# One order of the products for all wide weight chunks of a two-layer hybrid encoder trunk

## The chip, the cores and the metric

The kernel runs on one core of a Trainium2 chip. The metric is the device time of one execution in microseconds (us), taken as the median over several runs. The engines are TensorE (PE, with its weight loads PEld), VectorE (DVE), ScalarE (ACT), GpSimd (POOL) and SyncE (SP, which issues most DMAs).

## What is computed

The reference is a trunk of two layers over 256 frames of width 2048, in float32:

```
for layer in range(2):
    h = rms_norm(x, norm_mix_w[layer]) * (1 + sc1) + sh1        # scale, shift, gate from mod_w[layer] and c
    if layer == 0:
        mix = gdn_attn_mixer(h, ...)     # gated DeltaNet heads and chunked band attention, one output product
    else:
        mix = mamba2_ssd(h, ...)         # projections, convolution, SSD scan over chunks, gate, output product
    x = x + g1 * mix
    h = rms_norm(x, norm_mlp_w[layer]) * (1 + sc2) + sh2
    a = relu(h @ mlp_w1[layer])          # 2048 -> 8192
    x = x + g2 * ((a * a) @ mlp_w2[layer])   # 8192 -> 2048
```

Every large product is a stream of float32 weights against the 256 frames.

## The kernel before

All activations stay on the chip; weights come from HBM in chunks of 128 x 2048 numbers (1 MB), one DMA each. A chunk and the activations are each split in two float32r parts, a high one (the rounded value) and a low one (the rest), and three partial products are summed: high x high, high x low and low x high. For a chunk, `loader` (L467) issues the DMA on SP, ACT casts each half of the chunk to its high part `wh`, and DVE subtracts to get the low part `wl` (`split`, L317). There are four buffers of `wh` and four of `wl`, which is two chunks.

There are three kinds of items. `b_item` and `a_item` serve projections of 512 columns of weights; in `a_item` the weights are the moving operand and all its products are 512 columns wide. `c_item` (L559) serves a *wide chunk*: 256 columns of weights by 8 K tiles of 128. In it the weights are stationary. The moving operand is the activations: high and low part side by side, 512 columns, for `wh` (the function `both`), and the high part alone, 256 columns, for `wl` (the function `low`). So a wide chunk is 2 column tiles x 8 K tiles = 16 products of 512 columns and 16 of 256. The two column tiles `ct` add up in two different PSUM banks of one tile `pw`; the eight K tiles come in two halves `hf` of four, and each half has its own `wh` and `wl`.

Wide chunks in order of time: 16 of the output product of layer 0, 128 of its MLP, 24 of the SSD mixer's projections, 16 of its output product, again 24 and 16, and 128 of the MLP of layer 1; 352 in all. Between the two groups of projections and the output products stand the gate blocks of the SSD mixer (`a_item`).

What sets the order of the work is the program's own text and then a scheduler. The text runs one item after the other; `emit` (L242) loads the next item's weights and then runs the pending item, whose `run` yields every eight products. At each yield, `tick` (L227) lets background tasks step (evictions, convolutions, the SSD scan) and issues a share of the modulation weights' work (`mod_job`, L419: a DMA and a DVE step of 2.3 us). A scheduler then moves instructions within each engine's stream by its own estimates; so another order on PE can also change the order on DVE and ACT.

Which order the 32 products of a wide chunk take is `self.order`. It is "tile" outside the MLPs; inside them `mlp` (L1344) sets it anew for each of the eight half stages of each layer from a table (L1349). With W for a product of 512 columns and L for one of 256:

```
tile        W L W L ... within one half and one column tile
tile pairs  W W L L ... within one half and one column tile
row         W W L L ... column tiles in turn
crossed     W and L of both column tiles mixed
half        8 W, 8 L, 8 W, 8 L; four K tiles of one column tile, then of the other
half rows   8 W, 8 L, 8 W, 8 L; column tiles in turn
chunk rows  16 W, 16 L; column tiles in turn
```

In the gate blocks of the SSD mixer, two groups of each four set `self.flip` (L1579), which takes the two frame halves, and so the two PSUM banks, in turn.

Of the kernel before, what the change touches and what calls it, by code (L numbers as in the profile page):

```python
# [18 lines left out]
P = 128  # L19
# [93 lines left out]
class Trunk:  # L113
# [8 lines left out]
    def __init__(self, tc, ctx, ins, out):  # L122
        self.tc, self.nc = tc, tc.nc
        self.i, self.out = ins, out
        self.n = 0
        pool = lambda name, bufs, **k: ctx.enter_context(tc.tile_pool(name=name, bufs=bufs, **k))
        self.cp = pool("cp", 1)
        self.raw_p = pool("rawp", 4)
        self.w_p = pool("wp", 4)
        self.u_p = pool("up", 18)  # L130
        self.s_p = pool("sp", 2)
        self.dram_p = pool("drp", 1, space=bass.MemoryType.DRAM)
        self.ps_g = pool("psg", 2, space=PSUM)
        self.ps_m = pool("psm", 4, space=PSUM)
        self.fast, self.bg, self.open = [], [], []
        self.fast_n, self.bg_n = 0.5, 0.5
        self.credit = self.fcredit = 0.0
        self.pending = None
        self.order, self.flip = "tile", False
        self.pin = self.still = 0  # L140
        self.ahead = None
        self.pin_mod = 0
        self.debt = self.rate = 0.0
        self.modgen = iter(())
# [377 lines left out]
    def a_item(self, ps, src, act, first, last, after=None, whole=False):  # L522

        load, ws = self.loader(src, whole)
        flip = self.flip and not whole

        def run():
            o_, (u, x) = ps(), act()
            for hf, (wh, wl) in enumerate(self.tiles(ws, 512)):
                if flip:  # L530
                    for k in range(2):
                        ka = hf * 2 + k
                        st, sp = first and ka == 0, last and ka == 3
                        T = [slice(t * P, t * P + P) for t in range(2)]
                        for n in range(3):
                            for t in range(2):
                                self.mmx(o_[t], u[hf][:, k, n // 2, T[t]], (wh, wl, wh)[n][:, k], st and n == 0, sp and n == 2)
                        yield
                    continue
# [19 lines left out]
    def c_item(self, ps, src, act, first, last, after=None):  # L559

        load, ws = self.loader(src)

        order = self.order

        def run():
            o_ = ps()
            halves = self.tiles(ws, 256)

            def both(ct, hf, k):
                u = act(2 * hf + k // 2)[:, k % 2]  # L570
                self.mmx(o_[:, ct].rearrange("p a t -> p (a t)"), halves[hf][0][:, k, ct * P : ct * P + P], u.rearrange("p a t -> p (a t)"),
                         first and hf == k == 0, last and hf == 1 and k == 3)

            def low(ct, hf, k):
                self.mmx(o_[:, ct, 1], halves[hf][1][:, k, ct * P : ct * P + P], act(2 * hf + k // 2)[:, k % 2, 0], False, last and hf == 1 and k == 3)

            def steps(order):

                if order == "tile":
                    return [[f(ct, hf, k) for k in range(4) for f in (W, L)] for hf in range(2) for ct in range(2)]  # L580
                if order == "tile pairs":
                    return [[f(ct, hf, k + n) for k in (0, 2) for f in (W, L) for n in range(2)] for hf in range(2) for ct in range(2)]
                if order == "row":
                    return [[f(ct, hf, k + n) for n in range(2) for f in (W, L) for ct in range(2)] for hf in range(2) for k in (0, 2)]
                if order == "half":
                    return [[f(ct, hf, k) for ct in range(2) for k in range(4)] for hf in range(2) for f in (W, L)]
                if order == "half rows":
                    return [[f(ct, hf, k) for k in range(4) for ct in range(2)] for hf in range(2) for f in (W, L)]
                if order == "chunk rows":
                    return [[f(ct, hf, k) for k in range(4) for ct in range(2)] for f in (W, L) for hf in range(2)]  # L590
                if order == "crossed":
                    res = []
                    for hf in range(2):
                        a = [f for k in range(4) for f in ([W(0, hf, k)] + ([L(1, hf, k - 1)] if k else []) + [W(1, hf, k), L(0, hf, k)])] + [L(1, hf, 3)]
                        res += [a[:8], a[8:]]
                    return res

            W = lambda *a: (both, a)
            L = lambda *a: (low, a)
            for step in steps(order):  # L600
                for f, a in step:
                    f(*a)
                yield
# [740 lines left out]
    def mlp(self, layer, acts, after=None):  # L1344
# [4 lines left out]
        orders = ((("row", "tile pairs"), ("half", "half rows"), ("chunk rows", "crossed"), ("tile", "row")),  # L1349
                  (("tile pairs", "half"), ("half rows", "chunk rows"), ("crossed", "row"), ("half rows", "tile pairs")))  # L1350
# [14 lines left out]
        for f in range(NF):  # L1365
            a = []
            self.order = orders[layer][f][0]
# [5 lines left out]
            self.order = orders[layer][f][1]  # L1373
# [5 lines left out]
        self.order = "tile"  # L1379
# [6 lines left out]
    def run(self):  # L1386
# [176 lines left out]
        for half in range(2):  # L1563
# [14 lines left out]
            for g in G:  # L1578
                self.flip = g % 4 > 1  # L1579
                self.a_block(i["w_sz"], SZ + g, acts, lambda ps, g=g: os_.__setitem__(g % 4, self.evac(self.ssd_gate(g, ps, ys[g]), 1)))  # L1580
            self.flip = False
# [75 lines left out]
```

## Time and profile before

| | |
|---|---|
| median of 3 runs | 2752.32 us (2750.8 to 2754.2) |
| the profiled execution | 2751.96 us |
| its span, first to last instruction | 2750.2 us |
| PE busy | 2678.6 us |
| DVE busy | 2154.5 us |
| ACT busy | 1323.7 us |
| HBM read | 675.33 MB |

The rows further down name an instruction by line, engine, operation and tiles, out<-in. `pw` is the PSUM tile of a wide chunk; `pg` that of the other items; `pm` holds small products. `u` are activations, `wh` and `wl` the two parts of weights, `mraw` modulation weights, `sE`, `scb`, `sxw` tiles of the SSD scan. Matmuls are pipelined: the duration of one is longer than the time until the next one starts, and their ends are modelled.

### The profile page before, as it was taken

Reading aid. Unit: us, or ns where it says so; the run is one execution under the profiler, and the core shown is the slowest. Engines: PE = TensorE matmul, PEld = TensorE weight load, DVE = VectorE, ACT = ScalarE, POOL = GpSimd, SP = SyncE. Lnnn points to the kernel's source line nnn. Section 1 sums busy time; section 2 is a strip of 40 time slices with the busy share of each in tenths; the row PEclk is TensorE's granted clock in tenths of the full one; section 3 lists DMA queues with packets and bytes.
Section 4 is the critical chain, followed back from the end, with each engine's and each line's share of the span. In section 5 each row is a group of like instructions: output and inputs, shape, how many; then the busy total and the mean of one; then the engine's idle time right before and its main releaser. Section 6 shows DMA issues by size and latency. Waiting matters only on the chain.

```text
span 2750.2 us, 39612 instructions
## 1 busy us (share of the span) xinstructions
PE 2678.6 (97%) x15610; PEld 2341.0 (85%) x15610; DVE 2154.5 (78%) x3211; ACT 1323.7 (48%) x1841; POOL 24.6 (1%) x98
## 2 busy tenths in 40 slices
PE   5999999999999999999999999999999999999999
PEld 5887989878888888888788888888878888888888
DVE  7998998988888888777889876898777755555555
ACT  3444454445355354454555544555445354354452
POOL 1000000000000000000000000000000000000000
PEclk9999999999999999999999999999999999999999
DMA  9986487869888888887456565656557755555554
GB/s 345 351 322 238 158 317 274 310 235 348 307 323 303 318 301 306 303 305 273 179 197 206 210 214 199 235 193 219 196 186 287 275 192 191 184 185 192 190 188 134
DMA packets 99306, 680.06 MB, mean 247 GB/s; under 512 B 11056, under 2 KB 12336, under 8 KB 18224
## 3 DMA queue, kind: packets, MB, share of 16 engines
q1 hardware_dynamic: 94224, 669.07, 67.3%
q10 hardware_dynamic: 4896, 8.46, 1.0%
q8 instruction: 123, 2.02, 0.3%
q14 instruction: 63, 0.52, 0.1%
HBM read 675.33 MB, written 2.16 MB: 246 GB/s over the span
## 4 chain that ended last, share of the span: by engine, by line
PE 91%; DVE 6%; ACT 1%; issue 1%; DMA 1%; ACTq 0%; SPq 0%; DVEq 0%
PE pw L309 71%; PE pg L309 13%; PE pm L312 4%; PE pm L309 3%; DVE mraw L433 2%; DVE wl L319 1%; PE pm L315 1%; DVE hf L750 1%; DVE u L753 0%; DVE u L1441 0%; DVE x L791 0%; ACT pm L904 0%; ACT wh L318 0%; DMA x<-in_x_dram 0%; DMA sd_rowd<-sd_rows 0%
## 5 line engine op out<-in xcount | busy, mean ns | idle before, releaser
L309 PE MATMUL pw<-u,wh 128*128 128x512 f32 x5632 | 1746.1, 397 | 9.2 <-DVE u L753 5.5
L318 ACT CAST wh<-raw 128x1024 fp32r<-128x1024 f32 x870 | 910.7, 1053 | 1097.7 <-PE pw L309 818.1
L319 DVE TENSOR_TENSOR wl<-raw,wh 128x1024 fp32r<-128x1024 f32 x870 | 1054.6, 1222 | 410.8 <-ACT wh L318 361.7
L309 PE MATMUL pw<-u,wl 128*128 128x256 f32 x5632 | 1185.4, 281 | 1.3 <-DVE wl L319 1.3
L309 PEld LDWEIGHTS pw<-u,wh 128*128 128x128 f32 x5632 | 990.4, 189 | 170.0 <-issue 10.6
L309 PEld LDWEIGHTS pw<-u,wl 128*128 128x128 f32 x5632 | 966.9, 190 | 93.9 <-DVE wl L319 2.6
L433 DVE SCALAR_TENSOR_TENSOR mraw<-mraw,crow 128x2048 f32<-128x2048 f32 x192 | 438.9, 2287 | 33.3 <-DMA mraw<-in_mod_dram 33.1
L309 PE MATMUL pg<-wh,u 128*128 128x512 f32 x864 | 269.7, 396 | 0.0
L791 DVE SCALAR_TENSOR_TENSOR x<-pw,mod,x 128x256 f32<-128x256 f32 x352 | 161.5, 480 | 70.1 <-PE pw L309 67.3
L309 PEld LDWEIGHTS pg<-wh,u 128*128 128x128 f32 x864 | 161.3, 188 | 31.9 <-issue 0.5
L309 PE MATMUL pg<-wl,u 128*128 128x512 f32 x432 | 159.9, 394 | 0.7 <-DVE wl L319 0.5
L309 PE MATMUL pg<-u,wh 128*128 128x256 f32 x672 | 124.6, 285 | 0.0
L309 PEld LDWEIGHTS pg<-u,wh 128*128 128x128 f32 x672 | 105.7, 192 | 0.3
L309 PEld LDWEIGHTS pg<-wl,u 128*128 128x128 f32 x432 | 81.2, 188 | 17.6 <-DVE wl L319 1.8
L309 PE MATMUL pg<-u,wl 128*128 128x256 f32 x336 | 95.2, 283 | 0.0
L309 PE MATMUL pm<-u,wh 128*128 128x256 f32 x256 | 47.7, 290 | 19.2 <-ACT wh L318 19.2
L309 PEld LDWEIGHTS pg<-u,wl 128*128 128x128 f32 x336 | 64.4, 192 | 0.1
L846 DVE SCALAR_TENSOR_TENSOR u<-pad,cst,u 128x256 f32<-128x256 f32 x144 | 61.3, 481 | 1.9 <-ACT u L840 1.8
L319 DVE TENSOR_TENSOR u<-rl,u 128x512 fp32r<-128x512 f32 x64 | 44.2, 690 | 21.6 <-ACT u L318 21.6
L309 PEld LDWEIGHTS pm<-u,wh 128*128 128x128 f32 x256 | 41.0, 198 | 20.2 <-ACT wh L318 20.0
L752 ACT ACTIVATE u<-hf,mod 128x256 fp32r<-128x256 f32 x64 | 29.8, 505 | 56.2 <-DVE hf L750 56.2
L1355 ACT COPY rs<-pw 128x512 f32<-128x512 f32 x64 | 37.3, 583 | 31.8 <-PE pw L309 31.8
(279 smaller groups left out, 1508.6 us busy)
## 6 DMA issues: line engine op xcount, KB each, us to landing
raw<-in_w_dram SPq DMA_DIRECT2D x256, 1024.0 KB, 5.0
mraw<-in_mod_dram SPq DMA_DIRECT2D x192, 1024.0 KB, 5.5
raw<-in_w_ab_dram SPq DMA_DIRECT2D x56, 1024.0 KB, 5.8
raw<-in_w_ssd_dram SPq DMA_DIRECT2D x48, 1024.0 KB, 4.9
raw<-in_w_sz_dram SPq DMA_DIRECT2D x32, 1024.0 KB, 4.9
raw<-in_wo_ssd_dram SPq DMA_DIRECT2D x32, 1024.0 KB, 4.8
raw<-in_wo_ab_dram SPq DMA_DIRECT2D x16, 1024.0 KB, 5.6
sE<-sd_rowd ACTq DMA_DIRECT2D x32, 256.0 KB, 5.0
```

The source lines that it names most:

```text
L309: self.nc.tensor.matmul(o, a, b, start=start, stop=stop, skip_group_check=True)
L312: self.nc.tensor.matmul(o, lhsT, rhs, start=True, stop=True, skip_group_check=True)
L315: self.nc.tensor.transpose(o, a, self.ident[:k, :k])
L318: a = self.nc.scalar.copy(hi, src)
L319: b = self.nc.vector.tensor_tensor(lo, src, hi.bitcast(F32), op=ALU.subtract)
L433: x = nc.vector.scalar_tensor_tensor(raw, raw, 1.0, self.crow, op0=ALU.mult, op1=ALU.mult, accum_out=t[:, f : f + 1])
L750: nc.vector.scalar_tensor_tensor(h[:, f], self.x[cb][:, ff], scale[:, col], r, op0=ALU.mult, op1=ALU.mult)
L752: nc.scalar.activation(hi, h[:, f], AF.Identity, bias=shift[:, col])
L791: nc.vector.scalar_tensor_tensor(x[:, 2 * b + f], ps[:, f, n], g[:, 2 * cb + f : 2 * cb + f + 1], x[:, 2 * b + f], op0=ALU.mult, op1=ALU.add)
L846: nc.vector.scalar_tensor_tensor(h, pad[:, f, 1 + q : 257 + q], w[:, q, j : j + 1], h, op0=ALU.mult, op1=ALU.add)
L1355: nc.scalar.copy(lo, ps[:, :, 1])
```

## The change

`self.order`, the table of orders and the other orders go; `c_item` writes one order out: for both halves of the chunk all products with `wh`, the two column tiles in turn, then all with `wl`. It still yields every eight products. `self.flip` goes too, so that the gate blocks all take the order that the other `a_item` products have.

```
     def c_item(self, ps, src, act, first, last, after=None):
...
         def run():
             o_ = ps()
             halves = self.tiles(ws, 256)
-            for step in steps(order):
-                for f, a in step:
-                    f(*a)
-                yield
+            for n in range(2):
+                for hf in range(2):
+                    for k in range(4):
+                        u = act(2 * hf + k // 2)[:, k % 2]
+                        sp = last and hf == 1 and k == 3
+                        for ct in range(2):
+                            w = halves[hf][n][:, k, ct * P : ct * P + P]
+                            if n == 0:
+                                self.mmx(o_[:, ct].rearrange("p a t -> p (a t)"), w, u.rearrange("p a t -> p (a t)"), first and hf == k == 0, sp)
+                            else:
+                                self.mmx(o_[:, ct, 1], w, u[:, 0], False, sp)
+                    yield
...
     def mlp(self, layer, acts, after=None):
...
-        orders = ((("row", "tile pairs"), ("half", "half rows"), ("chunk rows", "crossed"), ("tile", "row")),
-                  (("tile pairs", "half"), ("half rows", "chunk rows"), ("crossed", "row"), ("half rows", "tile pairs")))
...
-            self.order = orders[layer][f][0]
...
-            self.order = orders[layer][f][1]
...
             for g in G:
-                self.flip = g % 4 > 1
                 self.a_block(i["w_sz"], SZ + g, acts, lambda ps, g=g: os_.__setitem__(g % 4, self.evac(self.ssd_gate(g, ps, ys[g]), 1)))
```

The instructions on every engine are the same ones, and on SP and POOL they stand in the same order. Three places show what moves.

First PE at the start of the second MLP product of layer 0, the first half of its first chunk. Before ("tile pairs"), the first four K tiles; `u_933` and `u_943` hold two K tiles each, `wh_1028` and `wl_1029` are the first half's weights, `wh_1030` and `wl_1031` the second's:

```order
L309 MATMUL pw_1037_6514<-u_933_5877,wh_1028_6496 128x512 x2
L309 MATMUL pw_1037_6514<-u_933_5877,wl_1029_6497 128x256 x2
L309 MATMUL pw_1037_6514<-u_943_5923,wh_1028_6496 128x512 x2
L309 MATMUL pw_1037_6514<-u_943_5923,wl_1029_6497 128x256 x2
L309 MATMUL pw_1037_6514<-u_933_5877,wh_1028_6496 128x512 x2
```

and in the changed kernel, the whole chunk:

```order
L308 MATMUL pw_1037_6514<-u_933_5877,wh_1028_6496 128x512 x4
L308 MATMUL pw_1037_6514<-u_943_5923,wh_1028_6496 128x512 x4
L308 MATMUL pw_1037_6514<-u_959_6031,wh_1030_6500 128x512 x4
L308 MATMUL pw_1037_6514<-u_975_6132,wh_1030_6500 128x512 x4
L308 MATMUL pw_1037_6514<-u_933_5877,wl_1029_6497 128x256 x4
L308 MATMUL pw_1037_6514<-u_943_5923,wl_1029_6497 128x256 x4
L308 MATMUL pw_1037_6514<-u_959_6031,wl_1031_6501 128x256 x4
L308 MATMUL pw_1037_6514<-u_975_6132,wl_1031_6501 128x256 x4
```

The first product with a `wl` was the third of the chunk and is now the seventeenth.

Second DVE in the SSD mixer's first projections, where the first convolution's result `u_1896` is finished (L849 before, L812 now), with the tiles `sE` of the scan, which a DMA loads, beside it. Before:

```order
L319 TENSOR_TENSOR wl_1930_12723<-raw_1926_12716,wh_1929_12722 128x1024
L1214 TENSOR_TENSOR sd_dr_12638<-sd_e_12636,sd_dt_12553 128x64
L846 SCALAR_TENSOR_TENSOR u_1896_12513<-pad_1924_12685,cst_84,u_1896_12513 128x256 x6
L1255 TENSOR_SCALAR sE_1931_12750<-sE_1931_12750,sd_col_12632 128x128 x3
L1240 TENSOR_TENSOR scb_1936_12762<-pm_1935_12758,Umask_239 128x256
L1255 TENSOR_SCALAR sE_1931_12750<-sE_1931_12750,sd_col_12632 128x128
L1255 TENSOR_SCALAR sE_1932_12752<-sE_1932_12752,sd_col_12632 128x128
L849 SCALAR_TENSOR_TENSOR u_1896_12513<-cvt_1925_12686,u_1896_12513 128x512
```

and now:

```order
L809 SCALAR_TENSOR_TENSOR u_1896_12513<-pad_1924_12685,cst_84,u_1896_12513 128x256 x6
L318 TENSOR_TENSOR wl_1930_12723<-raw_1926_12716,wh_1929_12722 128x1024
L812 SCALAR_TENSOR_TENSOR u_1896_12513<-cvt_1925_12686,u_1896_12513 128x512
L1218 TENSOR_SCALAR sE_1931_12750<-sE_1931_12750,sd_col_12632 128x128 x2
L318 TENSOR_TENSOR wl_1942_12784<-raw_1940_12781,wh_1941_12783 128x1024
L1203 TENSOR_TENSOR scb_1936_12762<-pm_1935_12758,Umask_239 128x256
L318 TENSOR_TENSOR wl_1944_12788<-raw_1940_12781,wh_1943_12787 128x1024
L1218 TENSOR_SCALAR sE_1931_12750<-sE_1931_12750,sd_col_12632 128x128 x2
```

The last step of the convolution stood behind five steps on `sE` and stands ahead of them now, behind one subtraction of weights; two more subtractions now stand among the steps on `sE`.

Third DVE in the output product of layer 0, where the last two splits of activations (`u_796`, `u_797`) are made. Before:

```order
L319 TENSOR_TENSOR wl_788_4885<-raw_784_4878,wh_787_4884 128x1024
L319 TENSOR_TENSOR wl_793_4927<-raw_791_4924,wh_792_4926 128x1024
L319 TENSOR_TENSOR u_796_4934<-u_540_3466,u_796_4934 128x2x256
L319 TENSOR_TENSOR u_797_4935<-u_540_3466,u_797_4935 128x2x256
L319 TENSOR_TENSOR wl_795_4931<-raw_791_4924,wh_794_4930 128x1024
```

and now:

```order
L318 TENSOR_TENSOR wl_788_4885<-raw_784_4878,wh_787_4884 128x1024
L318 TENSOR_TENSOR u_796_4934<-u_540_3466,u_796_4934 128x2x256
L318 TENSOR_TENSOR u_797_4935<-u_540_3466,u_797_4935 128x2x256
L318 TENSOR_TENSOR wl_793_4927<-raw_791_4924,wh_792_4926 128x1024
L318 TENSOR_TENSOR wl_795_4931<-raw_791_4924,wh_794_4930 128x1024
```

One of the two subtractions ahead of the splits has moved behind them.

## Rows read from the trace of the kernel before

**Rows 1.** The page: busy time of the engines; the chain that ended last, by line.

```profile
PE 2678.6 (97%) x15610; PEld 2341.0 (85%) x15610; DVE 2154.5 (78%) x3211; ACT 1323.7 (48%) x1841; POOL 24.6 (1%) x98
...
PE pw L309 71%; PE pg L309 13%; PE pm L312 4%; PE pm L309 3%; DVE mraw L433 2%; DVE wl L319 1%; PE pm L315 1%; DVE hf L750 1%; DVE u L753 0%; DVE u L1441 0%; DVE x L791 0%; ACT pm L904 0%; ACT wh L318 0%; DMA x<-in_x_dram 0%; DMA sd_rowd<-sd_rows 0%
```

**Rows 2.** Windows: start:end, us; busy PE, PEld, DVE, ACT, POOL; PEclk, DMA share, GB/s.

```profile
505.83:561.29 55.46, 55.46 (x322) 48.49 (x321) 53.25 (x74) 24.08 (x26) 0.00 (x0) 1.00 0.95 339
607.17:662.90 55.73, 55.73 (x322) 48.63 (x321) 49.35 (x52) 32.37 (x44) 0.00 (x0) 1.00 0.94 357
...
795.43:862.47 67.04, 67.04 (x387) 58.99 (x386) 53.77 (x56) 38.45 (x49) 0.00 (x0) 1.00 0.82 306
862.47:951.85 89.38, 89.38 (x514) 78.66 (x513) 73.01 (x85) 35.91 (x37) 0.00 (x0) 1.00 0.84 312
951.85:1040.92 89.07, 89.07 (x514) 78.73 (x513) 70.56 (x74) 49.43 (x61) 0.00 (x0) 1.00 0.86 312
1040.92:1131.16 90.24, 90.24 (x514) 78.51 (x513) 73.80 (x86) 35.14 (x36) 0.00 (x0) 1.00 0.79 294
1131.16:1221.61 90.45, 90.45 (x514) 78.48 (x513) 72.32 (x76) 49.12 (x60) 0.00 (x0) 1.00 0.84 308
...
1375.00:1583.20 208.20, 204.51 (x1107) 174.21 (x1107) 187.78 (x389) 109.96 (x158) 0.93 (x9) 0.99 0.59 206
1607.03:1674.87 67.84, 67.84 (x387) 58.86 (x385) 46.67 (x58) 27.42 (x29) 0.10 (x1) 1.00 0.61 215
1674.90:1925.80 250.90, 250.34 (x1370) 213.64 (x1369) 216.09 (x413) 131.60 (x178) 0.83 (x8) 1.00 0.60 210
...
2386.94:2477.18 90.24, 90.24 (x515) 78.50 (x513) 50.35 (x51) 48.08 (x60) 0.00 (x0) 1.00 0.54 185
```

**Rows 3.** Timeline of PE in "chunk rows": start us, duration us, what.

```profile
951.85 3.82 PE L309 MATMUL pw<-u,wh 128*128 128x512 f32 x16
955.51 2.08 PE L309 MATMUL pw<-u,wl 128*128 128x256 f32 x16
```

**Rows 4.** Timeline of PE, output product of layer 0; in brackets idle time and releaser.

```profile
500.20 0.47 PE L309 MATMUL pw<-u,wh 128*128 128x512 f32 x1 [0.72 <-DVE u L319]
```

**Rows 5.** Timeline of PE at the start of layer 0's second MLP product.

```profile
682.67 0.59 PE L309 MATMUL pw<-u,wl 128*128 128x256 f32 x2 [0.53 <-DVE wl L319]
```

**Rows 6.** Timeline after a norm: layer 0's MLP, then the SSD mixer's start.

```profile
593.22 0.48 DVE L753 SCALAR_TENSOR_TENSOR u<-hf,mod,u 128x256 fp32r<-128x256 f32 x1
...
594.73 0.40 PE L309 MATMUL pw<-u,wh 128*128 128x512 f32 x1
...
601.95 0.51 PE L309 MATMUL pw<-u,wl 128*128 128x256 f32 x2 [0.78 <-DVE wl L319]
...
1325.97 0.48 DVE L753 SCALAR_TENSOR_TENSOR u<-hf,mod,u 128x256 fp32r<-128x256 f32 x1
...
1328.38 0.40 PE L309 MATMUL pw<-u,wh 128*128 128x512 f32 x1
```

**Rows 7.** Timeline of DVE and PE at the SSD mixer's first transposes, then a window.

```profile
1409.92 0.68 DVE L1255 TENSOR_SCALAR sE<-sE,sd_col 128x128 f32<-128x128 f32 x3 [3.74 <-DMA sE<-sd_rowd]
...
1412.42 2.36 DVE L319 TENSOR_TENSOR wl<-raw,wh 128x1024 fp32r<-128x1024 f32 x2
...
1411.98 0.44 PE L315 MATMUL pm<-ident,u 128*128 128x128 f32 x2 [3.64 <-DVE u L849]
...
1419.82 1.02 PE L312 MATMUL pm<-sxw,scb 128*128 128x512 f32 x2
...
1413.40:1416.70 3.30, 3.30 (x13) 2.82 (x12) 3.03 (x7) 2.02 (x5) 0.00 (x0) 0.50 0.25 45
```

**Rows 8.** Waits of ACT and of DVE: total us, times, longest us.

```profile
ACT wh L318 <- PE pw L309: 818.1, 525, 3.4
...
DVE wl L319 <- PE pw L309: 11.0, 9, 1.5
```

More of the change, by code (lines that the diff above doesn't have):

```diff
@@ L138, in __init__ @@
         self.pending = None
-        self.order, self.flip = "tile", False
         self.pin = self.still = 0
@@ L524, in a_item @@
         load, ws = self.loader(src, whole)
-        flip = self.flip and not whole
         def run():
@@ L529, in run @@
             for hf, (wh, wl) in enumerate(self.tiles(ws, 512)):
[L530 to L537, printed above, removed]
-                        yield
-                    continue
                 for n in range(4):
@@ L561, in c_item @@
         load, ws = self.loader(src)
-        order = self.order
         def run():
@@ L567, in run @@
             halves = self.tiles(ws, 256)
[L569 to L596, printed above, removed]
@@ L598, in run @@
-            W = lambda *a: (both, a)
-            L = lambda *a: (low, a)
-            for step in steps(order):
-                for f, a in step:
-                    f(*a)
-                yield
+            for n in range(2):
[10 more added lines that the diff above has]
+                    yield
@@ L1378, in mlp @@
                               lambda ps, cb, f=f: self.residual(ps, cb, ("mlp", layer), f == NF - 1, layer == 1 and f == NF - 1), f * 2)
-        self.order = "tile"
         self.drain(after)
@@ L1578, in run @@
             for g in G:
-                self.flip = g % 4 > 1
                 self.a_block(i["w_sz"], SZ + g, acts, lambda ps, g=g: os_.__setitem__(g % 4, self.evac(self.ssd_gate(g, ps, ys[g]), 1)))
-            self.flip = False
             self.drain()
```

## The prediction

> **What bounds the kernel now.** I read first the page's busy times and its chain of waits: TensorE (PE) is busy for 97% of the span, and 71% of the chain that ended last are the products of the wide chunks, pw on L309 [rows 1]. Next come stretches by window: in the middle of both MLPs, in the SSD mixer's output product and nearly in its projections PE has no gap, while DVE has room (70.56 of 89.07 us, 46.67 of 67.84) [rows 2]. So what counts first is the time from the start of one product to the start of the next, and the few places where PE stands still come second.
>
> A wide chunk is 32 products, 16 of 512 columns (W, with the high half of the weights, wh) and 16 of 256 (L, with the low half, wl). The kernel before runs each order of them somewhere, so its trace holds the price of each. A window that is a whole number of chunks long, divided by that number (the counts in the rows are a few higher, since products overlap the window's edges), gives per chunk [rows 2]: "tile" in layer 0's MLP 90.45 / 16 = 5.653 us, "crossed" 90.24 / 16 = 5.640, "half" 67.04 / 12 = 5.587, "half rows" 89.38 / 16 = 5.586, "row" 55.73 / 10 = 5.573, "chunk rows" 89.07 / 16 = 5.567. "Tile pairs" changes between W and L as often as "row", and is taken at its price. The order to come is "chunk rows" everywhere: 16 W in 955.51 - 951.85 = 3.66 us [rows 3], and 16 L in the rest, 1.91.
>
> Two things follow. Neighbours in different banks are worth nothing: "half" stays in one bank for four products in a row, "half rows" changes it each time, and both take 5.587. What costs is the change between W and L: two returns from L to W a chunk ("half") against one ("chunk rows") make 0.020 us, 16 ("tile") against one make 0.086. But "tile" also runs at 55.46 / 10 = 5.546 in the output product of layer 0 [rows 2], below all others; it falls into one of two rhythms, and only the slow one has something to give.
>
> **The change, part by part.** The sum starts from the profiled execution, 2751.96 us (its span, 2750.2, and 1.8 around it), 0.4 below the median of the runs, 2752.32.
>
> *The rhythm.* No product is added or dropped, so each chunk moves from its price to 5.567. MLP of layer 0: "tile" 16 x 0.086 = 1.4, "crossed" 16 x 0.073 = 1.2, "half" and "half rows" 32 x 0.020 = 0.6, "row" and "tile pairs" 48 x 0.007 = 0.3; together 3.5. MLP of layer 1: 1.2 for "crossed", 48 x 0.020 = 1.0, 48 x 0.007 = 0.3; 2.5. First output product of the SSD mixer, 67.84 / 12 = 5.653 [rows 2]: 16 x 0.086 = 1.4. The mixer's 48 projection chunks run "tile" too. 21 of them run without anything between their products, nearly all in the slow rhythm: 1.6. 27 have the mixer's small products between theirs, which start the rhythm anew; for these I take half of 27 x 0.086, 1.2. The two output products that run at 5.546 lose 0.02 in some 20 chunks and gain as much in the slow chunks at the second one's start: nothing. Sum: 10.2 us. Bounds: 9.0 (nothing from the interrupted chunks) and 11.4 (all of it).
>
> [...]
>
> *The a-blocks.* The flip is dropped in four gate blocks, all of whose products have 512 columns; there is no change of width to save, and the banks were worth nothing above. Zero; by the price of a chunk's only return from L to W, 0.02, sixteen such chunks bound it at 0.3 either way.
>
> *Waits that the order moves.* (1) In the output product of layer 0 PE idles 0.72 us for a split of activations on DVE [rows 4]; one of the two subtractions of weights ahead of it, 1.2 us, now comes after it: -0.7, bounds -0.7 and 0. (2) At the start of layer 0's second MLP product PE idles 0.53 us for wl after two W [rows 5]. The new order asks for wl only after 16 W: -0.5, bounds -0.5 and 0. (3) Starts after a norm: the first chunk eats activations while DVE makes them, and the new order asks for the last of its eight K tiles with all 16 L still to do. In layer 0's MLP that K tile is ready at 593.70; two W and 16 L behind it, 2.4 us, end at 596.1, where the second chunk now starts at 594.73: +1.4. In return the third chunk's wait for wl, 0.78 us idle and 0.95 from start to start, goes, and the second chunk's excess of 0.24: +0.2 net. At the SSD mixer's start the K tile is ready at 1326.45, and 1328.8 stands against 1328.38: +0.4, and as much is taken for layer 1 [rows 6]. Together +1.0, bounds 0 and +2.2.
>
> *The SSD mixer's first transposes.* DVE waits 3.74 us for sE's landing; behind that stands the last step of the first convolution (L849), and PE idles 3.64 us for it [rows 7]. In the changed program that step stands ahead of sE with one subtraction before it, so it ends near 1408.1 and PE goes on at once. What is late next is the product of sxw and scb: PE comes to it after 16 W, four transposes and 16 L, at about 1414.3, while sxw stands on DVE behind ten steps on sE from 1409.92 (0.2 to 0.3 each), two subtractions (2.36), scb and five steps of a convolution (0.4 to 0.7 each), an estimate of 7.7 us: 1417.7. PE waits 3.4 us there and is still 2.1 ahead of 1419.82, where that product runs now [rows 7]. I take -2.1. Bounds: 0 (all given back) and -5.3 (no new wait, and the half clock behind the old one [rows 7], 3.3 us at half rate, gone too).
>
> *Buffers.* wh of a chunk's first half is freed 1.8 us into it instead of 2.8, wh of the second 3.7 instead of 5.6, wl of the first 4.6 instead of 2.8. Zero for this: ACT's casts wait 818.1 us in all for wh's release, DVE's subtractions only 11.0 for a release by PE [rows 8].
>
> Sum: 2752.0 - 10.2 - 0.7 - 0.5 + 1.0 - 2.1 = **2739.5 us**.
>
> **Rivals.** *A: the rhythm belongs to the place.* The interval is set by what runs beside PE (DMA, casts, evictions) and not by the order. Then every stretch keeps its time and only the waits move: 2752.0 - 2.3 = 2749.7. For it: "tile" has two prices. Against it: "crossed" takes 90.24 us in layer 1 as in layer 0, though DMA is busy 0.54 there and 0.79 here [rows 2]. [...] Chance 0.05.
>
> *B: DVE's new order takes the gain back.* Some 220 of DVE's rows move by a place or three, most in the SSD mixer's projections, where DVE is busy for 187.78 of 208.20 and 216.09 of 250.90 us [rows 2]. A step on sE that falls behind a subtraction is 1.2 us later. There are 8 groups with 4 products on sE each; a quarter of them late by 1 us make 8 us: 2747.5. For it: DVE has little room. Against it: PE loses 3.69 and 0.56 us in these stretches now, the first of them to the wait above. Chance 0.11.
>
> *C, slower: wl is held too long.* In the 48 projection chunks DVE's subtraction into the first wl buffer may start 4.6 us into the chunk instead of 2.8. If DVE waits for the release and not for the cast, it loses up to 48 x 1.8 = 86 us, less its idle 20 + 35 there: +31, or 2773 with the rhythm's gain. It decides from where the 11.0 us of [rows 8] grow beyond that idle time. Against it: the stretch of "chunk rows" has no gap at all [rows 2]. Chance 0.03.
>
> **How the numbers follow.** The forecast has 0.81. Its bounds give 2733 (the SSD wait and its half clock gone, the full rhythm) and 2747 (no wait gained, all starts worse, a rhythm of 9.0 and a little of B). The rivals hold the other 0.19, so the range is 2733 to 2747. About 0.2%, 5.5 us, is what a measurement of this kernel can tell from no change. Faster than 2746.8: the forecast and the better third of B, 0.85. Within 0.2%: A and the rest of B, 0.12. Slower: C, 0.03.
>
> **What would show it.** Right: 89.07 us for 16 chunks in every MLP stretch and 5.57 a chunk in the output products; no 3.64 us at the transposes, but some 3 us ahead of sxw's product; no wait for wl at the second MLP product. Wrong: stretches that keep 5.64 or 5.65, PE waiting for sE or sxw in many places, or DVE waiting for PE ahead of wl.

## Result, and the profile after

| | before | changed |
|---|---|---|
| median | 2752.32 us (2750.8 to 2756.2, 5 runs) | 2736.78 us (2735.76 to 2737.6, 5 runs) |
| profiled execution: span | 2750.2 us | 2734.1 us |
| mean granted clock of PE | 0.995 | 0.990 |

The ratio is 0.9941, 95% interval [0.9927, 0.9956]: 15.5 us faster, where 12.5 were forecast (2739.5, range 2733 to 2747).

The page of the changed kernel, against [rows 1]: PE's busy time went from 2678.6 to 2664.7 us, 13.9 of the 16.1 us of the span.

```profile
PE 2664.7 (97%) x15610; PEld 2345.0 (86%) x15610; DVE 2134.4 (78%) x3211; ACT 1319.8 (48%) x1841; POOL 24.3 (1%) x98
```

The windows of the changed kernel that answer to [rows 2], in its columns: two MLP products of layer 0 (they were "crossed" and "tile"), 12 chunks of the SSD mixer's first output product, a product of layer 1 ("crossed"), and the two stretches of projections and gate blocks, each whole.

```profile
1036.94:1126.00 89.06, 89.06 (x514) 78.70 (x513) 73.45 (x88) 36.08 (x36) 0.00 (x0) 1.00 0.85 307
1126.00:1215.07 89.07, 89.07 (x514) 78.73 (x513) 70.26 (x74) 49.21 (x60) 0.00 (x0) 1.00 0.84 307
1594.29:1661.09 66.80, 66.80 (x386) 59.03 (x386) 45.63 (x58) 27.49 (x29) 0.10 (x1) 1.00 0.63 225
2372.21:2461.28 89.07, 89.07 (x514) 78.72 (x513) 47.85 (x51) 48.73 (x60) 0.00 (x0) 1.00 0.55 186
1313.56:1571.00 257.44, 256.59 (x1413) 220.18 (x1414) 237.95 (x471) 144.38 (x209) 1.24 (x12) 0.99 0.60 210
1661.09:1911.39 250.30, 249.15 (x1370) 213.78 (x1370) 215.88 (x414) 128.33 (x177) 0.82 (x8) 1.00 0.60 209
```

90.24 and 90.45 us became 89.06 and 89.07; 67.84 became 66.80 (5.567 a chunk); the DMA share differs between layers 0 and 1 as before, and the price does not.

The timeline of PE in the changed kernel, at the places of [rows 5], [rows 6] and [rows 7], and one place more in the second half of the SSD mixer:

```profile
586.69 5.38 PE L308 MATMUL pw<-u,wh 128*128 128x512 f32 x14 [1.84 <-DVE u L716]
592.79 0.73 PE L308 MATMUL pw<-u,wh 128*128 128x512 f32 x2 [0.73 <-DVE u L716]
593.37 2.07 PE L308 MATMUL pw<-u,wl 128*128 128x256 f32 x16
595.27 3.82 PE L308 MATMUL pw<-u,wh 128*128 128x512 f32 x16
...
680.55 3.94 PE L308 MATMUL pw<-u,wh 128*128 128x512 f32 x16 [1.62 <-ACT wh L317]
...
1401.08 0.60 PE L314 MATMUL pm<-ident,u 128*128 128x128 f32 x4
...
1407.52 1.02 PE L311 MATMUL pm<-sxw,scb 128*128 128x512 f32 x2
...
1778.79 1.10 PE L311 MATMUL pm<-sxw,scb 128*128 128x512 f32 x2 [1.00 <-ACT cvt L811]
```

What is no longer there: the wait of 0.53 for wl behind the first products at 680.55, the 3.64 us at the transposes, and the half clock behind either. (The mean granted clock fell all the same, from 0.995 to 0.990: this profile ran at 0.50 from 13.2 to 43.9 us, where the one of before ran at 1.00. PE is busy for 6.6 of these 30.7 us in both, and the stretch up to the first output product is not longer.) What was expected and did not come: a wait ahead of the product of sxw at 1407.52. What came unannounced: 1.00 us at 1778.79, where the same product waits in the second half of the mixer.

Stretch by stretch, from the first product of one to the first of the next in the two traces (us), with the forecast of the prediction's terms:

| stretch | before | after | change | forecast |
|---|---|---|---|---|
| up to the first output product | 487.0 | 486.4 | -0.6 | 0 |
| output product, layer 0 | 100.6 | 100.3 | -0.3 | -0.7 |
| MLP, layer 0 | 732.8 | 726.9 | -5.8 | -3.8 |
| SSD projections and gates, both halves | 513.8 | 507.7 | -6.2 | -4.5 |
| first SSD output product | 91.6 | 90.1 | -1.5 | -1.4 |
| second SSD output product | 101.4 | 101.3 | -0.1 | 0 |
| MLP, layer 1 | 717.9 | 716.0 | -1.9 | -2.1 |
| end | 5.1 | 5.5 | +0.3 | 0 |

The first line is no effect: later profiles have 485.9 to 489.2 there, whichever kernel.

### The profile page after: what moved, and what is told of

Same layout as the page of the kernel before. It is cut to its first block, busy times and chain, and to the rows that moved or that the text cites. A ratio compares the mean times of both kernels' runs of the same rounds, so it can differ in the third digit from the quotient of the medians.

```text
span 2734.1 us, 39611 instructions
## 1 busy us (share of the span) xinstructions
PE 2664.7 (97%) x15610; PEld 2345.0 (86%) x15610; DVE 2134.4 (78%) x3211; ACT 1319.8 (48%) x1841; POOL 24.3 (1%) x98
## 4 chain that ended last, share of the span: by engine, by line
PE 91%; DVE 6%; ACT 1%; DMA 1%; issue 1%; SPq 0%; ACTq 0%; DVEq 0%
PE pw L308 71%; PE pg L308 13%; PE pm L311 4%; PE pm L308 2%; DVE mraw L432 2%; PE pm L314 1%; DVE wl L318 1%; DVE hf L713 1%; DMA raw<-in_w_ab_dram 1%; DVE u L716 0%; ACT wh L317 0%; DVE x L754 0%; DVE u L1399 0%; ACT pm L867 0%; DMA x<-in_x_dram 0%
## 5 line engine op out<-in xcount | busy, mean ns | idle before, releaser
L318 DVE TENSOR_TENSOR wl<-raw,wh 128x1024 fp32r<-128x1024 f32 x870 | 1043.1, 1219 | 454.4 <-issue 259.6
L308 PE MATMUL pw<-u,wh 128*128 128x512 f32 x5632 | 1359.4, 393 | 10.4 <-DVE u L716 7.5
L308 PEld LDWEIGHTS pw<-u,wh 128*128 128x128 f32 x5632 | 1037.0, 189 | 219.4 <-issue 9.7
L308 PEld LDWEIGHTS pw<-u,wl 128*128 128x128 f32 x5632 | 722.6, 191 | 27.0
L308 PE MATMUL pw<-u,wl 128*128 128x256 f32 x5632 | 735.1, 283 | 0.0
L308 PE MATMUL pg<-wh,u 128*128 128x512 f32 x864 | 280.4, 397 | 0.0
L308 PE MATMUL pg<-wl,u 128*128 128x512 f32 x432 | 170.3, 394 | 0.6 <-DVE wl L318 0.5
L1317 DVE TENSOR_TENSOR rs<-pw,rs 128x512 f32<-128x512 f32 x64 | 43.8, 684 | 3.4 <-ACT rs L1316 3.4
```

The costliest lines, as they stand in the source:

```text
L308: self.nc.tensor.matmul(o, a, b, start=start, stop=stop, skip_group_check=True)
L318: b = self.nc.vector.tensor_tensor(lo, src, hi.bitcast(F32), op=ALU.subtract)
L1317: nc.vector.tensor_tensor(lo, ps[:, :, 0], lo, op=ALU.add)
```

## The experiments

Two theories stood against each other at first. Mine: each chunk has the price of its order, set by the returns from products of 512 columns behind products of 256, and the waits belong to their places. The rival: the gain hangs on something that reaches across stretches (DVE's order in the SSD mixer, the DMA load), or on the PSUM banks that the change speaks of.

### The two halves of the change apart

The kernel before, with the new order in the MLPs alone, then everywhere but there:

```
-        orders = ((("row", "tile pairs"), ...
+        orders = ((("chunk rows",) * 2,) * 4,) * 2
```

```
-        self.order, self.flip = "tile", False
+        self.order, self.flip = "chunk rows", False
...
-        self.order = "tile"
+        self.order = "chunk rows"
         self.drain(after)
```

> The kernel before, with the new order in the chunks of both MLPs alone; the mixers keep their order by tile and the flip. If each stretch has its own price (the order sets the rhythm, and a wait belongs to the stretch it stands in), the MLPs give what they gave in the full change: layer 0 went from 732.8 to 726.9 us, layer 1 from 717.9 to 716.0, so 7.8 us in all and 2752.3 - 7.8 = 2744.5, with 89.07 us for 16 undisturbed chunks. If the rhythm belongs to the place, the rows of the mixers had to move too for it, and it stays within 1 us of 2752.3. If the gain of the full change came from the SSD mixer's new order of DVE alone, likewise.

> The other half: the kernel before, with the new order everywhere but in the MLPs' chunks (the flip stays). If the parts add up: 2752.3 less the 8.3 us that the stretches outside the MLPs gave in the full change, 2744.0, with the SSD mixer's first transposes free of the 3.64 us wait and of the half clock behind it, and the first output product of that mixer at 5.567 us a chunk. If the two halves hang together (the SSD mixer's order on DVE depends on what the MLP left), the 3.64 us stay or come back as a wait for the product of sxw, and the time is near 2752.3 - 3 = 2749.

Measured: 2744.37 (ratio 0.9971 [0.9959, 0.9982]) and 2744.19 (0.9971 [0.9959, 0.9982]). The two gains, 8.1 and 8.3 us against 2752.46, make 16.4, and the whole change 15.5. They add up within the uncertainty. In the first, the mixer kept its stop at the transposes; in the second, it was gone while the MLPs' chunks kept their old prices. That the rhythm belongs to the place (rival A) is out.

### Same bank for three of four neighbours

```
-                    for k in range(4):
-                        u = act(2 * hf + k // 2)[:, k % 2]
-                        sp = last and hf == 1 and k == 3
-                        for ct in range(2):
+                    for ct in range(2):
+                        for k in range(4):
+                            u = act(2 * hf + k // 2)[:, k % 2]
+                            sp = last and hf == 1 and k == 3
```

> The changed kernel with one loop turned: the four products of a half's tile 0 come first, then the four of tile 1, so that three of four neighbours write the same PSUM bank; 16 of 512 columns still stand ahead of 16 of 256. If bank neighbours are worth nothing and only the returns from 256 to 512 columns are: 5.567 us a chunk and 2736.8, within 1 us. If the banks carry the gain: up to the 5.65 of the order by tile, 352 x 0.08 = 28 us more, 2765.

Measured: 2740.45 (0.9958 [0.9945, 0.9970]); span 2736.6, 2.5 above the changed kernel's. Neither number came. In its profile, first the window of an undisturbed MLP product:

```profile
1126.64:1215.71 89.07, 89.07 (x515) 78.72 (x514) 70.14 (x74) 49.23 (x60) 0.00 (x0) 1.00 0.83 306
```

and then the timeline of PE at the start of layer 0's MLP:

```profile
586.19 1.62 PE L308 MATMUL pw<-u,wh 128*128 128x512 f32 x3 [1.85 <-DVE u L716]
588.34 3.78 PE L308 MATMUL pw<-u,wh 128*128 128x512 f32 x8 [0.53 <-DVE u L716]
592.30 1.69 PE L308 MATMUL pw<-u,wh 128*128 128x512 f32 x5 [0.18 <-DVE u L716]
...
595.75 3.82 PE L308 MATMUL pw<-u,wh 128*128 128x512 f32 x16
```

The banks cost nothing: 89.07 again. What is dearer is the three starts after a norm, where the first chunk takes 9.56, 9.29 and 9.30 us against 8.58, 8.60 and 8.60. That is 2.4 of the 2.5 us. When the last of the eight K tiles is there, five products with `wh` are still to do (the row at 592.30), and two in the changed kernel (its row at 592.79); three more at 0.23 us are 0.7. The wait of 0.53 for the fourth K tile is not the price, since the wait for the last one shrinks from 0.73 to 0.18. At layer 0's MLP some 0.3 more is half clock, which lasted to 592.9 there and to 590.1 in the changed kernel. So taking the column tiles in turn is worth something for the order of the K tiles, not for the banks.

### The flip put back

```
+        flip = self.flip and not whole
...
+                if flip:
...
+                        for n in range(3):
+                            for t in range(2):
+                                self.mmx(o_[t], u[hf][:, k, n // 2, T[t]], (wh, wl, wh)[n][:, k], st and n == 0, sp and n == 2)
```

> The changed kernel with the flip put back in the two last gate blocks of each half of the SSD mixer. By the prediction the a-blocks are worth nothing: 2736.8, within 0.5 us, and the time between the gate blocks' first and last product the same to 0.3 us. If the flipped order (neighbours in two banks) was a gain that the change gave up, the time falls below 2736.

Measured: 2736.94 (0.9944 [0.9930, 0.9958]). The two stretches from the last wide chunk before the gate blocks to the output product are 0.04 and 0.02 us shorter than without the flip (105.91 against 105.95, 107.07 against 107.09). Dropping the flip cost nothing that counts.

### One product of layer 0's MLP alone

```
-        orders = ((("row", "tile pairs"), ...
+        orders = ((("row", "chunk rows"), ...
```

> The kernel before with a single stretch changed: the 16 chunks of layer 0's first w2 product take the new order in place of pairs by tile. In the full change this stretch went from 91.7 to 89.2 us, where the prediction had a wait of 0.53 and 16 x 0.007 of rhythm, 0.6 in all. Theory: the half clock of 682.9 to 686.3 stands behind that wait, and goes with it; then the stretch gives 2.5 here too, and TensorE's clock is full through it: 2752.3 - 2.5 = 2749.8. Rival: the half clock comes from what the first w1 product's order left, which is not changed here; then it stays, the stretch gives 0.6 and the time is 2751.7.

Measured: 2750.62 (0.9991 [0.9982, 1.0000]), between the two numbers; the stretch itself decides. It takes 89.2 us, as in the full change (91.7 before). Windows from the product's start, of the kernel before and then of this one, where the second window is used further down:

```profile
681.41:686.91 5.50, 4.97 (x18) 3.96 (x19) 4.81 (x5) 4.86 (x7) 0.00 (x0) 0.69 0.93 322
```

```profile
684.05:689.55 5.50, 5.50 (x31) 4.83 (x32) 4.80 (x5) 5.44 (x8) 0.00 (x0) 1.00 0.95 340
1605.39:1671.95 66.56, 66.56 (x387) 58.19 (x385) 46.76 (x58) 27.49 (x29) 0.10 (x1) 1.00 0.62 219
```

PEclk is 0.69 in the mean in the one (0.50, 1.2 of 2.4 GHz, for 3.4 us of it) and 1.00 in the other. In both, PE had stood for 1.6 us for a cast just before; only the kernel before stands again, 0.53 us, shortly after. All five profiles with the wait for wl at this place (before and four experiments) show the lower clock behind it, and all five with the new order of 16 and 16 here, and no such wait, show 1.00. Removing half a microsecond of wait gave 2.4 of the 2.5 us.

### Head and tail of the SSD mixer's first projections

The new order in the first 8 chunks alone, then in the other 16 alone:

```
+                self.order = "chunk rows"
                 conv_block(SB_)
                 conv_block(SC_)
+                self.order = "tile"
```

```
             ys = {}
+            self.order = "tile" if half else "chunk rows"
...
+            self.order = "tile"
             os_ = {}
```

> The kernel before with the new order in the SSD mixer's first 8 chunks alone (its B and C projections); the 16 chunks behind them, in which the small rows are stored and read back and TensorE then stands for 3.64 us, keep theirs. Theory: the store of the rows took 5.2 us to land before and 2.2 after, since the order of the chunks around it sets when a weight load starts beside it; here that order is the old one, so the store takes about 5, DVE waits 3 to 4 us for sE, and the gain is 8 x 0.086 less the dearer start (0.6): nothing, 2752. Rival: being a little earlier is enough; then the store lands in about 2, the wait is gone, and the time is some 5 less, 2747.

> The other 16 chunks of that half, alone. Theory: the store lands in about 2.2 us, DVE's wait for sE and TensorE's 3.64 us go, and the half clock behind it too: 2752.3 - 3.64 - 1.7 and some 0.3 of rhythm, 2746.7. Rival (the head of the stretch decides): the store takes 5, the wait stays, 2752.

Measured: 2753.01 (1.0000 [0.9991, 1.0009]) and 2747.44 (0.9978 [0.9969, 0.9987]), both as my theory had it. The chain at stake runs through HBM: ACT copies the small rows out of PSUM, a DMA stores them (`sd_rowd`, 64 KB), and once that has landed the `sE` tiles are read back. From the answers on the tile `sd_rows`: the store's row and its time to landing, in the kernel before and in the changed one.

```profile
L1201 ACTq DMA_DIRECT2D sd_rowd<-sd_rows x1: 663/663/663, 1399.2 to 1399.2; - x1
...
DMA to landing us min/median/max: 5.2/5.2/5.2
```

```profile
L1164 ACTq DMA_DIRECT2D sd_rowd<-sd_rows x1: 664/664/664, 1391.3 to 1391.3; - x1
...
DMA to landing us min/median/max: 2.2/2.2/2.2
```

And what the DMA engines did meanwhile, in windows of 1 us (before, then after; the last two columns are DMA share and GB/s):

```profile
1400.00:1401.00 1.00, 1.00 (x7) 0.86 (x7) 1.00 (x4) 0.00 (x0) 0.00 (x0) 1.00 0.50 90
1401.00:1402.00 1.00, 1.00 (x9) 0.92 (x9) 0.52 (x1) 0.64 (x1) 0.00 (x0) 1.00 0.86 352
1402.00:1403.00 1.00, 1.00 (x7) 0.88 (x7) 0.55 (x1) 1.00 (x4) 0.00 (x0) 1.00 1.02 434
```

```profile
1391.00:1392.00 1.00, 1.00 (x6) 0.53 (x5) 0.86 (x1) 0.72 (x2) 0.00 (x0) 1.00 0.00 0
1392.00:1393.00 1.00, 1.00 (x7) 0.91 (x8) 0.89 (x2) 0.31 (x1) 0.00 (x0) 1.00 0.76 131
```

Before, the store shares the DMA engines with a weight load of 1 MB at up to 434 GB/s; after, they are idle when it is issued. With the head alone changed it lands in 4.9 us and PE stands 3.17 us at the transposes; with the tail changed, in 2.2, and nobody waits. Over all 14 profiles, the five with the old order in these 16 chunks have 4.9 to 5.3 us, a DVE wait for sE of 3.1 to 3.7 and the lower clock behind it; the nine others 2.1 to 2.2 and none of it at this place. In all five, 375 to 436 GB/s are moved in the third and fourth microsecond behind the store's issue; in all nine the DMA engines are idle in the first. (DVE does wait for other `sE` tiles in the second half of the mixer, in the changed kernel 2.24 us at 1732.34 where before had 0.22; PE does not stand there.)

The run with the head alone does not test the rival of an earlier store, since its store came 78.8 us into the stretch, as before. Other profiles do: in the same-bank run the store came at 78.3 us and took 2.2, in the run with one product changed at 78.0, earlier, and took 4.9. The landing goes with the order of these chunks in all 14, and not with the time.

Was it the landing, or the new order on DVE that stood in the order lists? In a later run (joined pairs in the MLPs, below) DVE has five steps on sE ahead of the convolution's last step (`u<-cvt,u`), as in the kernel before:

```profile
1399.72 1.06 DVE L1244 TENSOR_SCALAR sE<-sE,sd_col 128x128 f32<-128x128 f32 x5
1400.70 0.68 DVE L838 SCALAR_TENSOR_TENSOR u<-cvt,u 128x512 f32<-128x512 f32 x1
1401.30 0.47 DVE L1244 TENSOR_SCALAR sE<-sE,sd_col 128x128 f32<-128x128 f32 x2
```

No bracket, no wait: sE had landed. With an early landing DVE's order did not matter here. Why the order of the chunks brings the load's start away from the store was not traced to one buffer.

### Every chunk by tile

```
-        orders = ((("row", "tile pairs"), ...
+        orders = ((("tile",) * 2,) * 4,) * 2
```

> The kernel before with every chunk by tile, the order with the most returns from 256 to 512 columns (16 a chunk). If the order sets the rhythm, the undisturbed MLP stretches all go to one of the two rhythms of this order: 90.45 us for 16 chunks (all of them: 2752.3 + 256 x 0.086 - 6.0 = 2768), or 88.73 (all of them: 2741). If the place sets it, the stretches that ran in other orders keep 89.1, 89.2, 89.4 or 90.2 us, and the time stays within 1 us of 2752.3.

Measured: 2754.98, but over ten runs from 2745.58 to 2769.19 (1.0015 [0.9997, 1.0032]); the kernel before spread over 2749.1 to 2757.5 in 33 runs, the changed one over 1.8 us in 5. Two MLP products of 16 chunks, of layer 0 and of layer 1, by window:

```profile
952.80:1041.55 88.75, 88.75 (x514) 77.56 (x513) 70.80 (x74) 48.93 (x60) 0.00 (x0) 1.00 0.84 315
2298.52:2388.97 90.45, 90.45 (x515) 78.48 (x513) 52.13 (x62) 35.86 (x36) 0.00 (x0) 1.00 0.53 187
```

Both rhythms are there in one execution, and each holds until PE stops, other products come between, or the alternation itself is broken: in layer 1's first product of this run the slow rhythm follows the fast one at 2042.37, where two products of 512 columns stand in a row and PE did not stop. Nor do they belong to a place: the SSD mixer's first output product took 67.84 us for 12 chunks in the profile of before [rows 2] and 66.56 in the run with one product changed (above), where its code is the same; layer 0's output product ran at 5.547 in the profile of before and at 5.65 in this run and in the one with the mixer's tail changed. So "tile" has one of two prices, 5.547 or 5.653, and what chooses was not found. No other order showed two in the 14 profiles.

### Fewer returns still: joined pairs, and cheaper starts

The products of the two chunks of one output tile in one run of 32 W and one of 32 L, with six wl buffers; then, besides, the first two chunks at each start by K row (W W L L for each K tile):

```
             for hf in range(2):
                 part(0, hf)
                 yield
+            if late is not None and first:
+                late.append(part)
+                return
+            for f in (late or []) + [part]:
+                for hf in range(2):
+                    f(1, hf)
+                    yield
```

```
+            if rows:
+                for ka in range(8):
...
+                    for n in range(2):
+                        for ct in range(2):
```

> The changed kernel with the products of the two chunks of one output tile joined: 16 + 16 of 512 columns, then 16 + 16 of 256, so one return from 256 to 512 columns in two chunks; this takes six wl buffers in place of four, and 17 small buffers in place of 18 to make room. 304 of the 352 chunks are joined. If the return is what costs (0.020 us each, from two returns a chunk at 5.587 against one at 5.567), a joined pair takes 2 x 5.567 - 0.020 = 11.113 us, and the kernel 2736.8 - 304 x 0.010 = 2733.7. If the price hangs on the change of chunk and buffer and not on the return, the pair keeps 11.133 and the time 2736.8. If wl, held up to 7.3 us longer, makes DVE late, there are new waits for wl and the time is above 2737.

> The same, and at the three starts after a norm that open an MLP or the SSD mixer the first two chunks go by K row (two products of 512 columns and two of 256 for each K tile), so that little is left to do when the last K tile comes. The first four chunks took 24.84 us in the kernel before at layer 1's MLP and 25.32 after, 24.93 and 25.34 at the SSD mixer; at layer 0's MLP the first three took 19.52 and 19.72. If the dearer starts come from the 16 products of 256 columns that wait behind the last K tile: 0.2, 0.4 and 0.5 come back, 1.1 less than the run beside this one, near 2732.6. If DVE's splits ahead of the second and third chunk set them, the first chunk gets shorter, the third waits for wl, and the sum of the first four stays.

Measured: 2739.82 (0.9950 [0.9936, 0.9963]) and 2739.68 (0.9953 [0.9940, 0.9965]): no gain. But the price of a return between long runs is confirmed. In the first of the two, a window of 16 joined chunks, and the timeline of PE in the first block of another product of layer 1:

```profile
2288.49:2377.40 88.91, 88.91 (x515) 78.75 (x514) 52.76 (x62) 35.86 (x36) 0.00 (x0) 1.00 0.56 190
```

```profile
2118.91 1.21 PE L308 MATMUL pw<-u,wh 128*128 128x512 f32 x4 [1.32 <-DVE u L318]
```

88.91 / 8 = 11.114 us a pair, where 11.113 was expected from one return less. The gain went in part to new waits like the second row: the second chunk of a block now starts 3.7 us after the first and not 5.6, and at the head of a w2 product its activations are not split yet. The mixer's second projections and gates took 1.4 us more, of which a row names 0.5 (a wait at the transposes); the rest was not traced. The starts by K row did what was expected at layer 1's MLP (24.80 against 25.34 us for four chunks in the run beside it) and in the mixer (24.96 against 25.29).

So a last pair of kernels joined only where nothing had waited, or changed the starts alone:

```
-        late = [] if len(cbs) == 1 else None
+        late = [] if join else None
```

> Joined pairs only where the run before had no new wait: in the MLPs' blocks of one output tile, but not in the first w1 product of a layer and not in the first block of each w2 product, and nowhere in the mixers: 184 chunks; with the K rows at the three starts. If the joined pairs lost their gain to the waits at the first w2 blocks (6.4 us in place of 3.8 in layer 1) and in the mixer: 184 x 0.010 = 1.8 and the starts' 1.1 come through, 2736.8 - 2.9 = 2733.9. If the six wl buffers and the seventeen small ones cost by themselves, it stays above 2736.

> The changed kernel with the first two chunks at the three starts by K row, and nothing else. From the pairs run: 0.4 at the SSD mixer, 0.5 at layer 1, 0.2 at layer 0: 2735.7. If DVE's splits set the starts, nothing: 2736.8.

Measured: 2737.15 (0.9938 [0.9925, 0.9950]) and 2738.72 (0.9938 [0.9925, 0.9952]). Neither is told apart from the changed kernel. Each lost its gain mainly in one place. With the starts alone, the first w2 product of layer 0 begins 3.00 us late instead of 1.62 and then runs at half clock (timeline of PE, then window):

```profile
683.33 6.74 PE L308 MATMUL pw<-u,wh 128*128 128x512 f32 x16 [3.00 <-ACT wh L317]
```

```profile
683.30:687.30 4.00, 3.97 (x9) 3.14 (x10) 3.88 (x4) 3.97 (x6) 0.00 (x0) 0.50 0.63 219
```

With the pairs in the MLPs, the same wait comes, and the clock stays (timeline, then window); further on, DVE takes a modulation step of 2.29 us ahead of a split, PE stands for 1.85, and the clock is 0.50 for 3.4 us behind it:

```profile
680.69 3.96 PE L308 MATMUL pw<-u,wh 128*128 128x512 f32 x16 [3.00 <-ACT wh L317]
...
869.03 1.20 PE L308 MATMUL pw<-u,wh 128*128 128x512 f32 x4 [1.85 <-DVE u L318]
```

```profile
680.70:684.70 4.00, 4.00 (x18) 3.31 (x19) 3.87 (x4) 3.97 (x6) 0.00 (x0) 1.00 0.71 248
```

No version here beats the changed kernel.

## Why the prediction was right, and where it missed

**The rhythm** (-10.2): right in size, and right in that each order but "tile" has one price wherever it runs. The undisturbed stretches all went to 5.567 us a chunk. MLP of layer 0: the six stretches behind the first two gave 547.3 - 543.9 = 3.4 of the 3.5; MLP of layer 1: 1.9 net of 0.5 at its start, of 2.5; the first SSD output product 1.5, of 1.4. The undisturbed projection chunks gave 1.6, as forecast; the interrupted ones, read chunk by chunk without the waits, some 0.7 where half of the bound, 1.2, was taken. That bank neighbours cost nothing is shown by the same-bank run. What the prediction read as a property of two output products, their 5.546, was one draw of two; here it cost nothing, since it fell the same way for the term. There was luck in it: 5.6 of the 10.2 (1.4, 1.4, 1.6 and 1.2) price "tile" in the slow rhythm that the profile of before happened to show. In the run with one product changed, the same code ran fast in nearly all of the mixer's undisturbed projections and in most of its first output product.

The reason given, "what costs is the change between W and L", holds in part. The joined pairs show 0.020 us for a return between long runs of one width. But the number of returns does not make the price: "row" and "tile pairs" have eight a chunk and take 5.573, less than "half" with two (5.587), and "tile" in its fast rhythm has sixteen and takes 5.547, the least of all [rows 2]. The sum did not suffer, since it priced each chunk by its order. The times from one product's start to the next show where the 0.020 lies. In the changed kernel (1126.01 to 1215.07, means of 16 chunks) a W settles at 227 ns and an L at 120, which is 5.547 for 16 of each. Behind the return the first five W take 233, 236, 228, 232 and 231, and behind the change to L the first two take 113 and 119: 20 ns more in all. In runs of two ("row") the same difference is 3 ns a return, and in the alternation of "tile" 0 or 7. What happens in the engine there no run shows.

The Trainium skill (TensorE: Matmul & The Clock Gate, "Back-to-back issue gap") gives an isolated warm product its columns at 2.4 GHz plus about 2.5 ns, and says that in a stream in which each has its weight load both set the spacing. By the first alone, as an estimate, a chunk would take 5.20 us. No order here comes down to that: 5.547 is the least, and the same products take up to 5.653.

**The a-blocks** (0): right, 0.06 us in all by the flip put back.

**Waits.** (1) The wait for the split in layer 0's output product went, but the first chunk took 7.22 us instead of 6.77 and the later ones 5.567 instead of 5.547: -0.3 of -0.7. (2) At the second MLP product of layer 0, "-0.5" was the step that missed most after the next one: the half clock behind the wait, 3.4 us at half rate, is 1.7 us, and the stretch gave 2.5. The prediction priced a half clock at the transposes and overlooked the one here. (3) The starts: forecast +0.2, +0.4 and +0.4; measured +0.2 for the first three chunks at layer 0 (19.52 to 19.72, the first one 1.5 dearer), and +0.6 and +0.5 for the first chunk of the other two. Right in sum, but the old order varies there: the mixer's first four chunks took 24.6 to 25.7 us in five profiles with it, and 25.3 in five with the new one.

**The SSD mixer's first transposes** (-2.1, bounds 0 and -5.3): the wait went, but the term ended at its far bound; the two projection stretches gave 6.2 where the terms made 4.5, and the stall with the chunks beside it 5.4. The step that failed is "sxw stands on DVE behind ten steps on sE from 1409.92": it kept sE's landing where it was. sE's first step ran 89.5 us after the stretch's start before and 85.9 after, because the rows were stored 1.1 us earlier in the stretch and the store landed in 2.2 us instead of 5.2. So no wait took the place of the old one, and no half clock followed. A DMA's landing was treated as a constant of the trace, while the change moved the transfers beside it.

**The rivals.** A is out, by the two halves. B may be there in small: the 1.00 us ahead of sxw in the second half of the mixer, one place and not eight. The profile names ACT's `cvt` as what ended that wait; DVE's `sxw`, which the product reads, ended 0.13 us before it, behind six steps of a convolution. Which of them it waited for is not settled. C did not come: DVE's waits for a release by PE ahead of wl grew from the 11.0 us of [rows 8] to 76.8, but no wide chunk of PE waits for wl any more.

**The range.** The bounds of the terms add up to 2733.8 at the low end, where 2733 is given; it changes nothing.

## What to carry to other kernels

Price each order of a stream of products by a stretch that runs in it; here neither the count of width changes nor the banks would have given the price. Among the orders with a single price, the one with the longest runs of one width was the cheapest. But stop where the next operand is not ready: below one return a chunk, what was left to gain (0.010 us a chunk) did not come through. Price a short wait of PE with the clock that follows it, and look at what a small transfer meets on the DMA engines before taking its landing as fixed. An order with two rhythms shows one of them in a profile; compare the same stretch over several before calling it a price.

## What the runs showed of the hardware that was not expected

- Alternating products of 512 and 256 columns run at 5.547 or at 5.653 us for 32, on the same code and place, with a choice that holds until PE stops or the sequence is broken; a kernel made of them spread over 24 us in ten runs. What chooses was not found.
- In long runs a product of 512 columns settles at 227 ns and one of 256 at 120; behind a change of width the first five of 512 are up to 9 ns slower and the first of 256 is 7 ns faster, 20 ns net in the changed kernel.
- PE stood for 3.00 us at the same place in two kernels; behind it the granted clock was 0.50 in one and 1.00 in the other. The length of a wait alone does not tell whether the clock falls.
- A store of 64 KB took 2.2 us to land beside idle DMA engines and about 5 beside a weight load.
